# A hybrid decoder layer on one core: expert products in program order, the T5 bias as one row per head, and three more weight chunks requested under the output projection

## The chip, the cores and the metric

The kernel runs on one core of a Trainium2 chip and works in float32 from input to output. The metric is the device time of one execution in microseconds (us): the median of three runs before the change is 1792.37 us (1790.39 to 1792.63). One further execution was recorded by the profiler; it took 1793.54 us, and its recorded span is 1791.8 us. Engines are written as in the profile: PE (TensorE), DVE (VectorE), ACT (ScalarE), POOL (GpSimd), and SP, whose queue issues nearly all loads.

## The reference, cut to what matters

The layer computes 256 tokens plus 16 meta tokens of width 2048:

```python
h = layer_norm(concat([meta, x]))
(mq, mk, mv, mo, mi, mf, aq, ak, av, iq, ik, iw, gm, ga) = split_cols(h @ w_in)
qk = silu(causal_dwconv(concat([mq, mk])))
y_m = mlstm_branch(qk, mv, mo, mi, mf)          # 4 heads
# 8 heads; an indexer keeps 68 keys of 272 for each query
logits = q @ k_sel * scale + rel_bias[t5_bucket(q_pos - sel)]
y_a = softmax(logits) @ v_sel
merged = sigmoid(gm) * (y_m @ w_pm) + sigmoid(ga) * (y_a @ w_pa)
h = layer_norm(ALPHA * h + merged @ w_out)
# 4 groups of 8 experts: one group per token, the two best experts in it
gu = h[tokens of e] @ w_gate_up[e];  y += gate * ((silu(gu[:512]) * gu[512:]) @ w_down[e])
h = layer_norm(ALPHA * h + y);  return h[16:]
```

All 32 experts get their weights read: per expert 8 MB of w_gate_up and 4 MB of w_down.

## The kernel before, in words

**Stages.** In microseconds of the span: the embedding norm and the q/k projections of the mLSTM branch to about 100, the rest of the mLSTM branch to about 180, the indexer and the attention heads to about 400, merge gates and branch projections to about 700, the output projection w_out from 704 to 802, routing to 815, the experts from 815 to 1742, and the last norm to the end.

**Projections.** `fgroup` (L240 ff.) computes 256 columns of a projection. For every 8 rows of 128 it loads 1 MB (`load_w`, L114, on SP, tiles qk_r, mv_r, ...; three tiles in turn), ACT rounds the weights to a high part (L122, qk_00h), DVE takes the rest (L123, qk_00l), and PE multiplies (L261 for high parts, L267 for low). A tile is loaded again when ACT and DVE are done with the load three before it. `bg` is a list of generators: each `step()` moves the first two of them on by one piece, so that small work stands between projections.

**The T5 bias.** `t5_bias` computes for each of 8 heads a row of 400 bias values, in rsb (8 partitions). A DMA on POOL's queue (L310) writes every row 128 times to the DRAM tile rdr. `t5_load` reads it back on SP (L315) with a step of 399 between partitions, so that partition p gets the row shifted by p: the bias matrix Wb, 128 x 272 per head. `attend` adds the mask to Wb on POOL (L565).

**Expert weights.** `specs` lists the transfers of the experts in order: for each pair of experts 16 gate-up chunks of 1 MB, and 8 down chunks of 1 MB of the pair before; `issue(n)` requests the next ones as far as tiles are free or until n are requested. There are 12 free tiles under the output projection (NSLOT), 2 chunks in the tile acc0, and 2 in the tiles of u, which come free when ul is computed. From then on a chunk's tile is given back when its last product is done (`used`). In the output projection, `issue` is called with 4, 6, 8, 8 after the four column blocks; the rest is requested behind it, at `issue(NSLOT + 2)` and `issue(NSLOT + 4)`.

**Experts.** `dispatch(q)` gathers the tokens of four experts by a product with a one-hot matrix (pxe, L1004; 16 row blocks k, each 4 products of 256 columns: two with the high part uh of the tokens, two with the low part ul) and scales them into xe (L1008 on ACT, L1011 on DVE). `up_chunk` has four products of 512 columns per chunk (gu, L1081 and L1083), `down_step` the products py (L1104), and `combine` the products pc (L1212) that add the gated rows to acc. A scheduler orders all instructions of an engine by their priority and readiness; instructions wrapped in `late(...)` keep their place in the program. Before, the expert products aren't wrapped.

The program's own lines of the parts that the change touches:

## Time and profile before

| | value |
|---|---|
| median of three runs | 1792.37 us |
| profiled execution | 1793.54 us |
| its span | 1791.8 us |
| PE busy | 1713.5 us, 96% |
| DVE, ACT, POOL busy | 705.9, 454.1, 115.5 us |
| DMA, mean over the span | 301 GB/s |
| read from HBM | 533.53 MB |

The busy share of PE is a count of recorded matmuls, whose ends are modelled; two matmuls into different column halves of the array overlap in the records. So a busy PE in the experts doesn't by itself say that PE sets the pace there; the DMA share of the same stretch has to be read beside it. The profile's sections give the span in 40 equal slices; the stretches below are finer.

### The profile page before, as it was taken

What the parts mean: (1) busy time and instruction counts of PE and PEld (TensorE: products, weight loads), DVE (VectorE), ACT (ScalarE), POOL (GpSimd) and SP (SyncE); (2) the same over time, 40 slices, a digit from 0 to 9 for tenths busy, and PEclk for the clock granted to TensorE, in tenths of its full rate; (3) what the DMA queues carried; (4) which work ended last, traced back from release to release, by engine and by line L of the source; (5) the groups of instructions that cost most, each with busy time, mean ns of one, the idle gap of its engine ahead of it and who ended that gap; (6) DMA issues with size and microseconds to landing.
All of it is one profiled execution on the core that took longest, in us unless ns stands there. A gap on an engine that the chain in (4) does not pass through costs nothing. (4 is left out here: it accounts for less than half of the span.)

```text
span 1791.8 us, 20692 instructions
## 1 busy us (share of the span) xinstructions
PE 1713.5 (96%) x8478; PEld 1053.3 (59%) x8478; DVE 705.9 (39%) x1180; ACT 454.1 (25%) x687; POOL 115.5 (6%) x139
## 2 busy tenths in 40 slices
PE   8599999999999999999999999999999999999996
PEld 7598899988877877885343443433434434334332
DVE  7356774455456466543123123321222122112215
ACT  5143344444443444334010100100101001001011
POOL 3000200001032022000100000000000000000002
PEclk9799999999998999998999999999999999999998
DMA  7634444447565558648999999999999999999994
GB/s 221 124 124 143 142 154 153 142 149 245 194 196 163 188 189 306 209 168 324 416 393 421 420 419 420 419 419 420 419 419 420 420 419 420 420 420 419 420 411 138
DMA packets 156179, 538.68 MB, mean 301 GB/s; under 512 B 16012, under 2 KB 64356, under 8 KB 107936
## 3 DMA queue, kind: packets, MB, share of 16 engines
q1 hardware_dynamic: 153120, 530.54, 76.8%
q0 software_dynamic: 2896, 6.75, 2.0%
q8 instruction: 68, 1.11, 0.3%
q14 instruction: 31, 0.25, 0.0%
q10 hardware_dynamic: 64, 0.02, 0.0%
HBM read 533.53 MB, written 3.74 MB: 300 GB/s over the span
## 5 line engine op out<-in xcount | busy, mean ns | idle before, releaser
L1081 PE MATMUL gu<-weg,xe 128*64 128x512 f32 x1016 | 465.9, 598 | 0.6 <-DMA weg<-in_w_gate_up_dram 0.6
L1083 PE MATMUL gu<-weg,xe 128*64 128x512 f32 x1016 | 463.6, 598 | 0.0
L1104 PE MATMUL py<-wed,hT 128*64 128x512 f32 x960 | 308.6, 597 | 0.6 <-DMA wed<-in_w_down_dram 0.6
L1081 PEld LDWEIGHTS gu<-weg,xe 128*64 128x64 f32 x1016 | 126.7, 137 | 188.6 <-issue 181.8
L1104 PEld LDWEIGHTS py<-wed,hT 128*64 128x64 f32 x960 | 97.8, 137 | 160.5 <-issue 155.1
L1083 PEld LDWEIGHTS gu<-weg,xe 128*64 128x64 f32 x1016 | 122.3, 136 | 64.9 <-issue 62.7
L1089 ACT ACTIVATE hb<-gu 64x512 f32<-64x512 f32 x32 | 18.9, 592 | 471.4 <-PE gu L1083 471.4
L1090 DVE TENSOR_TENSOR hb<-gu,hb 64x512 f32<-64x512 f32 x32 | 22.0, 689 | 291.1 <-ACT hb L1089 290.5
L1231 DVE SCALAR_TENSOR_TENSOR yl<-py,gsl,yh 128x512 fp32r<-128x512 f32 (+1 forms) x65 | 46.5, 737 | 205.0 <-ACT yh L1230 205.0
L1230 ACT ACTIVATE yh<-py,gsl 128x512 fp32r<-128x512 f32 (+1 forms) x65 | 43.0, 680 | 273.9 <-PE py L1104 201.8
L1218 DVE TENSOR_TENSOR acc<-pc,acc 128x512 f32<-128x512 f32 (+1 forms) x122 | 79.4, 679 | 82.6 <-PE pc L1212 82.5
L1004 PE MATMUL pxe<-oh,uh 128*128 128x256 f32 x256 | 65.5, 333 | 9.0 <-DVE xe L1011 4.8
L1011 DVE TENSOR_SCALAR xe<-pxe,gbp 128x256 f32<-128x256 f32 x64 | 34.8, 544 | 92.4 <-PE pxe L1004 52.1
L1004 PEld LDWEIGHTS pxe<-oh,uh 128*128 128x128 f32 x256 | 40.8, 196 | 47.0 <-DVE xe L1011 15.8
L1204 POOL TENSOR_TENSOR fin<-acc,fin 128x512 f32<-128x512 f32 (+1 forms) x10 | 10.3, 1054 | 896.8 <-DMA wel<-in_w_down_dram 887.2
L1212 PE MATMUL pc<-yh,ohT 128*128 128x512 f32 (+1 forms) x130 | 55.8, 456 | 4.6 <-ACT yh L1230 2.4
L1212 PEld LDWEIGHTS pc<-yh,ohT 128*128 128x128 f32 x130 | 23.1, 191 | 55.5 <-issue 17.8
L1004 PE MATMUL pxe<-oh,ul 128*128 128x256 f32 x256 | 51.6, 284 | 0.0
L1008 ACT ACTIVATE xe<-pxe,gbp 128x256 f32<-128x256 f32 x64 | 36.1, 565 | 59.1 <-PE pxe L1004 58.9
L1212 PE MATMUL pc<-yl,ohT 128*128 128x512 f32 (+1 forms) x130 | 49.1, 405 | 0.8 <-DVE yl L1231 0.7
L1004 PEld LDWEIGHTS pxe<-oh,ul 128*128 128x128 f32 x256 | 40.8, 198 | 0.0
L1212 PEld LDWEIGHTS pc<-yl,ohT 128*128 128x128 f32 x130 | 24.1, 190 | 12.3 <-issue 8.1
(922 smaller groups left out, 3064.3 us busy)
## 6 DMA issues: line engine op xcount, KB each, us to landing
weg<-in_w_gate_up_dram SPq DMA_DIRECT2D x254, 1024.0 KB, 17.7
wed<-in_w_down_dram SPq DMA_DIRECT2D x120, 1024.0 KB, 16.7
gm_r<-in_w_in_dram SPq DMA_DIRECT2D x16, 1024.0 KB, 5.0
ga_r<-in_w_in_dram SPq DMA_DIRECT2D x16, 1024.0 KB, 5.1
wo_r<-in_w_out_dram SPq DMA_DIRECT2D x16, 1024.0 KB, 5.1
qk_r<-in_w_in_dram SPq DMA_DIRECT2D x8, 1024.0 KB, 6.0
mv_r<-in_w_in_dram SPq DMA_DIRECT2D x8, 1024.0 KB, 5.3
aq_r<-in_w_in_dram SPq DMA_DIRECT2D x8, 1024.0 KB, 5.1
```

Of the source, the lines that this page charges most:

```text
L1004: nc.tensor.matmul(pt[:, :4 * C], lhsT=part[:, b, rows_of(k)], rhs=ohf[:, b], start=i == 0 and b == 0, stop=i == 1 and b == 1)
L1008: nc.scalar.activation(xe[:, k], pt[:, :4 * C], AF.Identity, bias=gbp[:, 1, k:k + 1], scale=gbp[:, 0, k:k + 1])
L1011: nc.vector.tensor_scalar(xe[:, k], pt[:, :4 * C], gbp[:, 0, k:k + 1], gbp[:, 1, k:k + 1], op0=ALU.mult, op1=ALU.add)
L1081: nc.tensor.matmul(pg_[other], lhsT=lt, rhs=w[:, kk, 0:512], start=k == 0, stop=k == KD - 1)
L1083: nc.tensor.matmul(pg_[mine], lhsT=lt, rhs=w[:, kk, 512:1024], start=k == 0, stop=k == KD - 1)
L1089: nc.scalar.activation(hb[mine], pg_[other], AF.Silu)
L1090: nc.vector.tensor_tensor(hb[mine], pg_[mine], hb[mine], op=ALU.mult)
L1104: nc.tensor.matmul(py[i * 64:i * 64 + 64], lhsT=hTs[p][:, kk, 64 - i * 64:128 - i * 64], rhs=live["d", 2 * p + i, kk][:, 0, c * 512:c * 51 ...
L1212: nc.tensor.matmul(pc[:, :n], lhsT=ohT[:, b * P:b * P + P], rhs=y[:, :n], start=i == 0, stop=i == 1)
L1218: nc.vector.tensor_tensor(av, pc[:, :n], av, op=ALU.add)
L1230: nc.scalar.activation(yh[:, :n], py[:, :n], AF.Copy, scale=gate)
L1231: nc.vector.scalar_tensor_tensor(yl[:, :n], py[:, :n], gate, yh[:, :n].bitcast(F32), op0=ALU.mult, op1=ALU.subtract)
```

## The change

Five edits:

1. **T5 bias.** rdr holds one row of 400 per head (8 x 400). `t5_load` reads it with a step of one element between partitions, which gives Wb with its partitions in reverse order. A new generator `t5_flip` puts them right: a 128 x 128 matrix with ones on the other diagonal (`anti`), eight float32 products of 128 x 272, and eight copies on ACT back to Wb. It stands in `bg` behind the indexer.
2. **Weights.** A pool `pre` is opened before the output projection. It holds acc0 (chunks 0 and 1 of expert 1) and the tiles yh and yl, which take chunk 7 of expert 0 in four parts of 256 KB. `issue` is called with 4, 8, 10, 10 under the output projection, then NSLOT + 3 and NSLOT + 5.
3. **Dispatch.** Two row blocks share a PSUM bank (`bank`); for the first four experts only two banks are gathered before the first expert product, and one more behind each chunk. The first part of ul is computed on POOL, the others on DVE just before their bank.
4. **Order.** Every product and transpose of the experts is wrapped in `late`. A `combine` comes one step after the gating of its rows (`ready`).
5. **keep_warm** has 11 products instead of 14.

```diff
-    rdr = dram.tile([8, P, 400], F32, name="rdr")
+    rdr = dram.tile([8, 400], F32, name="rdr")
 
...
-        late(nc.gpsimd.dma_start(out=rdr, in_=rsb.unsqueeze(1).to_broadcast([8, P, 400])))
+        late(nc.gpsimd.dma_start(out=rdr, in_=rsb))
 
     def t5_load():
         rv = rdr[:]
         for h in range(0, AH, 2):
             late(nc.sync.dma_start(
                 out=Wb[:, h:h + 2],
-                in_=bass.AP(rv.tensor, rv.offset + h * P * 400 + 127,
-                            [[399, P], [P * 400, 2], [1, L]])))
+                in_=bass.AP(rv.tensor, rv.offset + h * 400, [[1, P], [400, 2], [1, L]])))
+
+    def t5_flip():
+        anti = ap_.tile([P, P], F32, name="anti")
+        nc.gpsimd.memset(anti, 0.0)
+        nc.gpsimd.affine_select(anti, anti, pattern=[[1, P]], compare_op=ALU.not_equal, fill=1.0,
+                                base=1 - P, channel_multiplier=1)
+        yield
+        for h in range(AH):
+            pw = pxt(f"pfl{h}")
+            nc.tensor.matmul(pw[:, :L], lhsT=anti, rhs=Wb[:, h], start=True, stop=True)
+            nc.scalar.copy(Wb[:, h], pw[:, :L])
+            yield
 
 
     qk = mp_.tile([P, 8, L], F32, name="qk")
@@ -605,6 +616,7 @@
             bg.append(g)
 
     bg.append(index_scores())
+    bg.append(t5_flip())
     for j in range(AH // 2):
+            nm = "we" + "_".join(map(str, key))
             if key in extra:
-                w = extra[key]().rearrange("p (a b) -> p a b", a=a)
+                live[key] = extra[key](nm, src)
+                continue
+            home[key] = pool, tag = free.popleft()
+            w = pool.tile([P, a, b], F32, name=nm, tag=tag, bufs=1)
+            nc.sync.dma_start(out=w, in_=src)
+            if key[0] == "g":
+                live[key] = lambda kk, h, w=w: w[:, kk, h * 512:h * 512 + 512]
             else:
-                home[key] = pool, tag = free.popleft()
-                w = pool.tile([P, a, b], F32, name="we" + "_".join(map(str, key)), tag=tag, bufs=1)
-            nc.sync.dma_start(out=w, in_=src)
-            live[key] = w
+                live[key] = w
 
     def used(*key):
     ta_ctx.close()
+    pre = ctx.enter_context(tc.tile_pool(name="pre", bufs=1, side="right"))
+    both = []
+
+    def in_acc(i, nm, src):
+        if not both:
+            both.append(pre.tile([P, 2, 2, 1024], F32, name="acc0", tag="acc"))
+        w = both[0][:, i]
+        nc.sync.dma_start(out=w, in_=src)
+        return lambda kk, h: w[:, kk, h * 512:h * 512 + 512]
+
+    def in_parts(nm, src):
+        ws = [pre.tile([P, 512], F32, name=f"{nm}{i}", tag=("yh", "yl")[i % 2], bufs=2)
+              for i in range(4)]
+        for i, w in enumerate(ws):
+            nc.sync.dma_start(out=w, in_=src[:, i // 2, i % 2 * 512:i % 2 * 512 + 512])
+        return lambda kk, h: ws[2 * kk + h]
+
+    extra.update({("g", 0, 7): in_parts, ("g", 1, 0): lambda *a: in_acc(0, *a),
+                  ("g", 1, 1): lambda *a: in_acc(1, *a)})
     free += [(big, t) for t in YT] + [(mx, t) for t in MT]
     NSLOT = len(free)
-        issue((4, 6, 8, 8)[n])
+        issue((4, 8, 10, 10)[n])
         for b in range(2):
             uv = u[b][:, sl]
             nc.vector.scalar_tensor_tensor(uv, uv, ALPHA, pts[b], op0=ALU.mult, op1=ALU.add)
...
     ul = me.tile([P, 2, D], F32R, name="ul", bufs=1)
-    both = []
-
-    def in_acc(i):
-        if not both:
-            both.append(me.tile([P, 2 * D], F32, name="acc0", tag="acc", bufs=1))
-        return both[0][:, i * D:i * D + D]
-
-    extra.update({("g", 1, NSLOT - 8 + i): lambda i=i: in_acc(i) for i in range(2)})
-    issue(NSLOT + 2)
+    issue(NSLOT + 3)
     free += [(up, t) for t in UT]
 
 
-    keep_warm(14, "warm1")
+    keep_warm(11, "warm1")
     mu1 = cst([P, 2, 2], "mu1")
     rs1 = cst([P, 2], "rs1")
     lg = cst([P, 2, 40], "lg")
...
 
+    def mm(*a, **k):
+        late(nc.tensor.matmul(*a, **k))
+
+    def turned(*a):
+        late(nc.tensor.transpose(*a))
...
         xe = me.tile([P, KD, 4 * C], F32, name=f"xe{q}", tag="xe", bufs=1)
         ohf = oh.rearrange("p b e c -> p b (e c)")
-        for k in range(KD):
-            if q == 0 and k % 4 == 0:
+
+        def bank(kc):
+            if q == 0 and kc % 2 == 0:
                 for b in R2:
-                    sl = slice(k * P, k * P + 512)
-                    nc.vector.tensor_tensor(ul[:, b, sl], u[b][:, sl],
-                                            uh[:, b, sl].bitcast(F32), op=ALU.subtract)
-            pt = pdt(f"pxe{q}_{k}")
-            for i, part in enumerate((uh, ul)):
-                for b in R2:
-                    nc.tensor.matmul(pt[:, :4 * C], lhsT=part[:, b, rows_of(k)],
-                                     rhs=ohf[:, b], start=i == 0 and b == 0,
-                                     stop=i == 1 and b == 1)
-            if k % 2:
-                nc.scalar.activation(xe[:, k], pt[:, :4 * C], AF.Identity,
-                                     bias=gbp[:, 1, k:k + 1], scale=gbp[:, 0, k:k + 1])
-            else:
-                nc.vector.tensor_scalar(xe[:, k], pt[:, :4 * C], gbp[:, 0, k:k + 1],
-                                        gbp[:, 1, k:k + 1], op0=ALU.mult, op1=ALU.add)
-        return xe, ohf
+                    sl = slice(kc * 256, kc * 256 + 512)
+                    if kc == 0:
+                        nc.gpsimd.tensor_tensor(ul[:, b, sl], u[b][:, sl],
+                                                uh[:, b, sl].bitcast(F32), op=ALU.subtract)
+                    else:
+                        late(nc.vector.tensor_tensor(ul[:, b, sl], u[b][:, sl],
+                                                     uh[:, b, sl].bitcast(F32), op=ALU.subtract))
+            pt = pdt(f"pxe{q}_{kc}")
+            for k in (2 * kc, 2 * kc + 1):
+                pv = pt[:, k % 2 * 256:k % 2 * 256 + 256]
+                for i, part in enumerate((uh, ul)):
+                    for b in R2:
+                        mm(pv, lhsT=part[:, b, rows_of(k)], rhs=ohf[:, b],
+                           start=i == 0 and b == 0, stop=i == 1 and b == 1)
+                if k % 2:
+                    nc.scalar.activation(xe[:, k], pv, AF.Identity, bias=gbp[:, 1, k:k + 1],
+                                         scale=gbp[:, 0, k:k + 1])
+                else:
+                    nc.vector.tensor_scalar(xe[:, k], pv, gbp[:, 0, k:k + 1],
+                                            gbp[:, 1, k:k + 1], op0=ALU.mult, op1=ALU.add)
+
+        for kc in range(2 if q == 0 else 8):
+            bank(kc)
+        return xe, ohf, bank
 
     def slots_of(q, ohf):
 
...
 
-    def flush(n=8):
-        for _ in range(min(n, len(pend))):
-            pend.pop(0)()
+    ready = []
+
+    def flush():
+
+        while ready:
+            ready.pop()()
+        if pend:
+            ready.append(pend.pop(0)())
 
     hTs = {}
 
...
-            yh = me.tile([P, 512], F32R, name=f"yh{nn}", tag="yh", bufs=2)
-            yl = me.tile([P, 512], F32R, name=f"yl{nn}", tag="yl", bufs=2)
+            yh = pre.tile([P, 512], F32R, name=f"yh{nn}", tag="yh", bufs=2)
+            yl = pre.tile([P, 512], F32R, name=f"yl{nn}", tag="yl", bufs=2)
             nc.scalar.activation(yh[:, :n], py[:, :n], AF.Copy, scale=gate)
             nc.vector.scalar_tensor_tensor(yl[:, :n], py[:, :n], gate, yh[:, :n].bitcast(F32),
                                            op0=ALU.mult, op1=ALU.subtract)
-            combine(nn, c0, n, yh, yl, cur[0][:, j], p == 0, p == LAST)
+            return lambda: combine(nn, c0, n, yh, yl, cur[0][:, j], p == 0, p == LAST)
         return gated
 
     turn = []
@@ -1244,6 +1291,8 @@
             if kc == 0:
                 pg_ = pgu.tile([P, 512], F32, name=f"gu{e}", tag="gu")
             up_chunk(e, kc, xe, pg_)
+            if p == 0 and n < 6:
+                bank(n + 2)
             while turn:
                 turn.pop()()
             for _ in range(0 if n == 0 else 1 if n < 15 else 2):
             if n == 10 and p % 2:
                 cur = slots_of(p // 2, ohf)
-            if len(pend) > 1 or n < 2:
-                flush(1)
+            flush()
             if n == 7:
                 hb = me.tile([P, 512], F32, name=f"hb{p}", tag="hb", bufs=1)
...
             for i in range(2):
-                nc.tensor.matmul(py[i * 64:i * 64 + 64, :n], lhsT=hTs[LAST][:, kk, 64 - i * 64:128 - i * 64],
+                mm(py[i * 64:i * 64 + 64, :n], lhsT=hTs[LAST][:, kk, 64 - i * 64:128 - i * 64],
                                  rhs=live["l", NE - 2 + i, c0][:, kk], start=kk == 0, stop=kk == 3)
-        gated(c0, n, py)
-    flush()
+        gated(c0, n, py)()
 
     mp_ctx.close()
 
```

Three places in the order of instructions, before and after.

SP's queue under the output projection, before; wo_r are the loads of w_out, weg chunks of w_gate_up, wed of w_down, acc the two chunks in acc0:

```order
L810 DMA weg_6_6649<-in_w_gate_up_dram 128x2048
L114 DMA wo_r_6361<-in_w_out_dram 128x4x512
L114 DMA wo_r_6411<-in_w_out_dram 128x4x512
...
L114 DMA wo_r_6785<-in_w_out_dram 128x4x512
L810 DMA weg_2_6857<-in_w_gate_up_dram 128x2048
L810 DMA weg_0_6853<-in_w_gate_up_dram 128x2048
L810 DMA weg_3_6859<-in_w_gate_up_dram 128x2048
L810 DMA weg_1_6855<-in_w_gate_up_dram 128x2048
L810 DMA weg_7_6651<-in_w_gate_up_dram 128x2048
L810 DMA acc_6861<-in_w_gate_up_dram 128x2048 x2
```

The same place of the changed kernel:

```order
L823 DMA weg_6_6515<-in_w_gate_up_dram 128x2048
L114 DMA wo_r_6393<-in_w_out_dram 128x4x512
L850 DMA weg_70_6517<-in_w_gate_up_dram 128x512
L114 DMA wo_r_6443<-in_w_out_dram 128x4x512
L850 DMA weg_71_6518<-in_w_gate_up_dram 128x512
...
L843 DMA acc_6691<-in_w_gate_up_dram 128x2048
L114 DMA wo_r_6477<-in_w_out_dram 128x4x512
L114 DMA wo_r_6531<-in_w_out_dram 128x4x512
L843 DMA acc_6691<-in_w_gate_up_dram 128x2048
...
L114 DMA wo_r_6826<-in_w_out_dram 128x4x512
L823 DMA weg_5_6900<-in_w_gate_up_dram 128x2048
```

Three chunks (one of them in four parts) have moved from behind the last wo_r load to between the earlier ones; five whole chunks stay behind it.

PE at the first expert products, before; pxe are the gathering products, gu the gate-up products:

```order
L1004 MATMUL pxe0_2_6980<-oh0_6962,ul_6852 128x256 x2
L1081 MATMUL gu0_7077<-weg_0_0_6305,xe0_6965 64x512
L1083 MATMUL gu0_7077<-weg_0_0_6305,xe0_6965 64x512
L1081 MATMUL gu1_7129<-weg_1_0_6853,xe0_6965 64x512
L1083 MATMUL gu1_7129<-weg_1_0_6853,xe0_6965 64x512
L1004 MATMUL pxe0_3_6986<-oh0_6962,uh_6851 128x256 x2
L1004 MATMUL pxe0_3_6986<-oh0_6962,ul_6852 128x256 x2
L1004 MATMUL pxe0_4_6994<-oh0_6962,uh_6851 128x256 x2
L1004 MATMUL pxe0_4_6994<-oh0_6962,ul_6852 128x256 x2
L1004 MATMUL pxe0_5_7000<-oh0_6962,uh_6851 128x256 x2
L1004 MATMUL pxe0_5_7000<-oh0_6962,ul_6852 128x256 x2
L1081 MATMUL gu0_7077<-weg_0_0_6305,xe0_6965 64x512
```

The same place of the changed kernel, where pxe0_1 is the second bank of two row blocks:

```order
L1007 MATMUL pxe0_1_7016<-oh0_6999,uh_6892 128x256 x2
L1007 MATMUL pxe0_1_7016<-oh0_6999,ul_6893 128x256 x2
L1007 MATMUL gu0_7034<-weg_0_0_6337,xe0_7002 64x512 x4
L1007 MATMUL pxe0_2_7041<-oh0_6999,uh_6892 128x256 x2
L1007 MATMUL pxe0_2_7041<-oh0_6999,ul_6893 128x256 x2
L1007 MATMUL pxe0_2_7041<-oh0_6999,uh_6892 128x256 x2
L1007 MATMUL pxe0_2_7041<-oh0_6999,ul_6893 128x256 x2
L1007 MATMUL gu0_7034<-weg_0_1_6339,xe0_7002 64x512 x4
```

The four products of a chunk now stand together, with one bank of eight gathering products between chunks; before, single products of two experts' chunks stood between gathering products.

PE at the end of the experts, before; ph are the transposes of the last pair, pc14 the combination of the pair before, pg broadcast rows, py15 the last pair's down products:

```order
L1083 MATMUL gu31_11137<-weg_31_7_11132,xe7_10725 64x512
L1096 MATMUL ph15_11249<-ident_63,hb15_11134 128x128 x4
...
L1296 MATMUL py15_0_11304<-wel_30_0_11144,hT15_11254 64x512
L1212 MATMUL pc14_15360_11272<-yh14_1536_11268,ohT7_11171 128x512
L1212 MATMUL pc14_15360_11272<-yl14_1536_11269,ohT7_11171 128x512
...
L1296 MATMUL py15_0_11304<-wel_31_0_11146,hT15_11254 64x512
L1296 MATMUL py15_512_11331<-wel_30_512_11148,hT15_11254 64x512
L1212 MATMUL pc15_00_11317<-yh15_0_11313,ohT7_11171 128x512
L1212 MATMUL pc15_01_11324<-yh15_0_11313,ohT7_11171 128x512
L1212 MATMUL pc15_00_11317<-yl15_0_11314,ohT7_11171 128x512
```

The same place of the changed kernel:

```order
L1007 MATMUL gu31_11108<-weg_31_7_11103,xe7_10708 64x512 x4
L1007 MATMUL py14_2_11009<-wed_28_3_11075,hT14_11021 64x512
...
L1007 MATMUL py14_3_11010<-wed_29_3_11077,hT14_11021 64x512
L1007 MATMUL pc14_5120_11210<-yh14_512_11198,ohT7_11142 128x512
...
L1010 MATMUL ph15_11224<-ident_63,hb15_11105 128x128 x4
L1007 MATMUL pc14_10240_11231<-yh14_1024_11218,ohT7_11142 128x512
...
L1007 MATMUL py15_0_11275<-wel_31_0_11117,hT15_11229 64x512
L1007 MATMUL pc15_00_11288<-yh15_0_11284,ohT7_11142 128x512
L1007 MATMUL pc15_00_11288<-yl15_0_11285,ohT7_11142 128x512
```

Four down products and four combination products of the pair before now stand behind the last gate-up chunk, and a block's down products no longer have other work between them.

## Rows read from the trace of the kernel before

**Rows 1.** The page's 40 slices of the span: GB/s

```profile
GB/s 221 124 124 143 142 154 153 142 149 245 194 196 163 188 189 306 209 168 324 416 393 421 420 419 420 419 419 420 419 419 420 420 419 420 420 420 419 420 411 138
```

**Rows 2.** Windows: stretch, its length, busy us (instructions) of PE, PEld, DVE, ACT, POOL, PEclk, DMA share, GB/s

```profile
1100.00:1300.00 200.00, 196.46 (x854) 81.04 (x852) 45.31 (x80) 22.28 (x37) 0.00 (x0) 1.00 1.01 419
```

**Rows 3.** PE in order of time from 1739 us: start, length, what

```profile
1741.71 0.59 PE L1081 MATMUL gu<-weg,xe 128*64 128x512 f32 x1
...
1742.14 0.59 PE L1081 MATMUL gu<-weg,xe 128*64 128x512 f32 x1
```

**Rows 4.** Windows before the experts

```profile
200.00:250.00 50.00, 48.82 (x385) 45.44 (x384) 40.91 (x96) 21.73 (x38) 5.03 (x9) 1.00 0.48 151
250.00:400.00 150.00, 150.00 (x1087) 140.72 (x1086) 73.94 (x146) 67.81 (x136) 9.84 (x15) 1.00 0.49 154
...
700.00:815.00 115.00, 110.96 (x541) 92.90 (x539) 66.79 (x106) 46.96 (x60) 11.59 (x7) 0.97 0.61 214
```

**Rows 5.** PE's waits from 40 to 130 us: total, times, longest

```profile
PE qk_p L261 <- ACT qk_00h L122: 20.3, 1, 20.3
```

**Rows 6.** ACT in order of time, 60 to 84 us: start, length, what [idle before]

```profile
82.05 1.04 ACT L122 CAST qk_00h<-qk_r 128x1024 fp32r<-128x1024 f32 x1 [24.77 <-DMA qk_r<-in_w_in_dram]
```

**Rows 7.** DMA issues from 40 to 60 us: count, KB, median us to landing

```profile
qk_r<-in_w_in_dram SPq DMA_DIRECT2D x3, 1024.0 KB, 32.5
rdr<-rsb POOLq DMA_DIRECT2D x1, 1600.0 KB, 37.6
```

**Rows 8.** DMA from 45 to 79 us: queue, packets, MB, share of 16 engines

```profile
q0 software_dynamic: 439, 1.58, 47.3%
```

**Rows 9.** DMA issues from 36 to 41 us

```profile
qk_r<-in_w_in_dram SPq DMA_DIRECT2D x1, 1024.0 KB, 5.3
mhg<-in_mh_norm_g_dram POOLq DMA_DIRECT2D x1, 512.0 KB, 3.7
```

**Rows 10.** Windows around the wait

```profile
50.60:62.70 12.10, 12.10 (x98) 12.04 (x96) 6.96 (x11) 3.16 (x5) 0.00 (x0) 1.00 0.63 94
62.70:83.15 20.45, 0.16 (x3) 0.00 (x1) 0.02 (x1) 1.10 (x2) 0.00 (x0) 0.57 0.58 109
83.15:98.08 14.93, 14.93 (x97) 14.93 (x97) 9.40 (x13) 5.51 (x7) 0.00 (x0) 0.79 0.57 181
```

**Rows 11.** DMA issues from 148 to 160 us

```profile
Wb<-rdr SPq DMA_DIRECT2D x4, 272.0 KB, 5.8
```

**Rows 12.** PE lines by form, 250 to 400 us: busy us, mean ns | idle

```profile
L567 PE MATMUL pl<-ak,aq 128*128 128x272 f32 x16 | 5.0, 392 | 0.0
```

**Rows 13.** Windows under the output projection and at the start of the experts

```profile
740.00:800.00 60.00, 60.00 (x294) 50.34 (x293) 29.22 (x31) 21.55 (x23) 0.00 (x0) 1.00 0.47 161
...
815.00:840.00 25.00, 24.32 (x120) 12.47 (x122) 9.03 (x23) 9.29 (x18) 0.00 (x0) 0.93 0.70 265
```

**Rows 14.** SP in order of time, 824 to 842 us

```profile
834.20 6.31 SPq L810 DMA_DIRECT2D weg<-in_w_gate_up_dram  x4
```

**Rows 15.** PE in order of time, 812 to 836 us

```profile
817.86 1.12 PE L1081 MATMUL gu<-weg,xe 128*64 128x512 f32 x1
...
820.66 0.51 PE L1004 MATMUL pxe<-oh,uh 128*128 128x256 f32 x2
...
825.44 0.51 PE L1004 MATMUL pxe<-oh,uh 128*128 128x256 f32 x2
...
826.59 0.64 PE L1083 MATMUL gu<-weg,xe 128*64 128x512 f32 x1
```

**Rows 16.** The DMA issued between 838.3 and 838.6 us

```profile
weg<-in_w_gate_up_dram SPq DMA_DIRECT2D x1, 1024.0 KB, 6.6
```

**Rows 17.** PE in order of time in the last block

```profile
1755.63 3.65 PE L1296 MATMUL py<-wel,hT 128*64 128x512 f32 x16
1760.06 0.73 PE L1212 MATMUL pc<-yh,ohT 128*128 128x512 f32 x2 [0.77 <-ACT yh L1230]
```

**Rows 18.** PE's waits from 840 to 1742 us, the longest

```profile
PE ph L1096 <- DVE hb L1090: 9.9, 7, 1.4
```

More of the change, by code (lines that the diff above doesn't have):

```diff
@@ L1021, in slots_of @@
         for j in range(2):
-            nc.tensor.matmul(pr[:, j * S:j * S + S],
+            mm(pr[:, j * S:j * S + S],
                              lhsT=sel[:, 2 * j:2 * j + 2].rearrange("p a b -> p (a b)"), rhs=rkT,
@@ L1030, in slots_of @@
             for b in R2:
-                nc.tensor.matmul(pgt[:, j * 4:j * 4 + 4], lhsT=ohf[:, b, j * P:j * P + P],
+                mm(pgt[:, j * 4:j * 4 + 4], lhsT=ohf[:, b, j * P:j * P + P],
                                  rhs=Gs[:, b, 2 * q + j], start=b == 0, stop=b == 1)
@@ L1080, in up_chunk @@
             lt = xe[:, k, s0:s0 + C]
-            nc.tensor.matmul(pg_[other], lhsT=lt, rhs=w[:, kk, 0:512], start=k == 0,
+            mm(pg_[other], lhsT=lt, rhs=w(kk, 0), start=k == 0,
                              stop=k == KD - 1)
-            nc.tensor.matmul(pg_[mine], lhsT=lt, rhs=w[:, kk, 512:1024], start=k == 0,
+            mm(pg_[mine], lhsT=lt, rhs=w(kk, 1), start=k == 0,
                              stop=k == KD - 1)
@@ L1095, in up_turn @@
         for kk in range(4):
-            nc.tensor.transpose(pt[:, kk * P:kk * P + P], hb[:, kk::4], ident)
+            turned(pt[:, kk * P:kk * P + P], hb[:, kk::4], ident)
         hT = me.tile([P, 4, P], F32, name=f"hT{p}", tag="hT", bufs=1)
@@ L1103, in down_step @@
         for i in range(2):
-            nc.tensor.matmul(py[i * 64:i * 64 + 64], lhsT=hTs[p][:, kk, 64 - i * 64:128 - i * 64],
+            mm(py[i * 64:i * 64 + 64], lhsT=hTs[p][:, kk, 64 - i * 64:128 - i * 64],
                              rhs=live["d", 2 * p + i, kk][:, 0, c * 512:c * 512 + 512],
@@ L1109, in down_step @@
                 used("d", 2 * p + i, kk)
-    xe, ohf = dispatch(0)
-    issue(NSLOT + 4)
+    xe, ohf, bank = dispatch(0)
+    issue(NSLOT + 5)
     acc = rkT = None
@@ L1120, in bcast_rows @@
         r = slice(32 * n, 32 * n + 9)
-        nc.tensor.matmul(pt, lhsT=dg[r], rhs=gr[r], start=True, stop=True)
+        mm(pt, lhsT=dg[r], rhs=gr[r], start=True, stop=True)
         return pt
@@ L1130, in prepare @@
         for b in R2:
-            nc.tensor.transpose(pt[:NE, b * P:b * P + P], rk[:, b], ident)
+            turned(pt[:NE, b * P:b * P + P], rk[:, b], ident)
         nc.vector.tensor_copy(rkT, pt[:NE, :S])
-        acc = me.tile([P, 2, D], F32, name="acc", tag="acc", bufs=1)
+        acc = pre.tile([P, 2, D], F32, name="acc", tag="acc")
     def add_residual(n):
@@ L1140, in add_residual @@
         for b in R2:
-            t = me.tile([P, 512], F32, name=f"rt{n}{b}", tag="yl")
+            t = pre.tile([P, 512], F32, name=f"rt{n}{b}", tag="yl", bufs=2)
             nc.vector.tensor_tensor(t, uh[:, b, sl].bitcast(F32), ul[:, b, sl].bitcast(F32),
@@ L1192, in rows_split @@
         nonlocal gr
-        h = me.tile([P, 512], F32R, name="grh", tag="yh")
+        h = pre.tile([P, 512], F32R, name="grh", tag="yh", bufs=2)
         gr = me.tile([P, 512], F32R, name="gr", bufs=1)
@@ L1211, in combine @@
             for i, y in enumerate((yh, yl)):
-                nc.tensor.matmul(pc[:, :n], lhsT=ohT[:, b * P:b * P + P], rhs=y[:, :n],
+                mm(pc[:, :n], lhsT=ohT[:, b * P:b * P + P], rhs=y[:, :n],
                                  start=i == 0, stop=i == 1)
@@ L1275, in trunk @@
                     turn.pop()()
-                flush()
+                while pend or ready:
+                    flush()
             if q + 1 < NE // 4:
-                xe, ohf = dispatch(q + 1)
+                xe, ohf, _ = dispatch(q + 1)
         if p == 1:
```

1 line of the change is left out of this document (removed).

## The prediction

> **What bounds the kernel now.** I read the GB/s slices first, then windows by stage, then the waits of each stage. The slices show two kernels in one [rows 1]: from about the 21st slice on the memory moves 419 to 421 GB/s without a gap, before that less than half of it mostly. In the experts the DMA share is 1.01 at 419 GB/s [rows 2]; 1 MB takes 1.0486 MB / 419 GB/s = 2.50 us. PE's busy share of 98% there misleads: two gate-up products into different halves start together and the next two 0.43 us later [rows 3], so four experts need 32 chunks x 4 + 16 down chunks x 4 = 192 pairs of products x 0.43 = 82.6 us, and with gathering (64 products, 9.2 us, from 8 in 1.15 us [rows 15]), combining (32 products at about 0.37 us [rows 17]) and some 3 us of small products about 107 us, while their 48 MB take 120 us. The reader is to see that the experts end when the last chunk has come, and that only an earlier start of the stream, or a shorter tail behind it, helps.
>
> Before the experts it is PE. Its windows are full or nearly so [rows 4], so what is cut from PE's path there moves everything behind it forward. The one large hole is early: PE waits once for 20.3 us [rows 5], for a cast on ACT, which itself waited 24.77 us for the load of qk_r [rows 6]. That load and its neighbours took 32.5 us (median of three), beside a write of rdr of 1600 KB that took 37.6 us [rows 7]. The write's queue held 47.3% of the 16 engines from 45 to 79 us while it moved 1.58 MB [rows 8]. A qk_r load just ahead of it landed after 5.3 us [rows 9].
>
> **The T5 edit: the stall.** The write shrinks from 1600 KB to 12.8 KB. The loads then take 5.3 us again [rows 9]: the load that ended at 82.05 was issued by 82.05 - 32.5 = 49.6 and lands by about 55, while PE has work until 62.7 [rows 10]. Gone are the idle 20.45 us, and the lower clock after it: the group that followed took 14.93 us at a granted clock of 0.79 where its like at 1.00 took 12.10 [rows 10], 2.83 us more. Together 23.3 us. What is late next would be ACT, DVE and SP; in the group before, ACT was busy 3.16 and DVE 6.96 of 12.10 us [rows 10], so neither takes the place of the load. If loads come a little late all the same, as much as 4 us of the 23.3 stays; that is the bound I keep for this term, apart from the rivals.
>
> **The T5 edit: the read and the flip.** Wb is read as before with four DMAs of 272 KB, which landed in 5.8 us [rows 11]. They now read all rows from one 12.8 KB block. The nearest row is mhg, 512 KB fetched from a row of 4 KB for each of 128 partitions, in 3.7 us [rows 9], so I take no loss. [...]
>
> The flip adds eight float32 products of 128 x 272 on PE, which stand one by one between projections. The attention's pl products of this shape and type were recorded as 16 records, two each, and 5.0 us of busy time [rows 12], 0.62 us for one. That is eight of them: 5.0 us at most, less what their ends overlap with the next product; I take 4.4. Below, nothing, if they fall into the idle 1.2 us of 200 to 250 and into other waits [rows 4]; above, 6.3, with one wait of 1.3 us for a copy. The eight copies on ACT are hidden: ACT is busy 21.73 of 50 us there. The memset and select on POOL (5.03 of 50 busy) too; if Wb came late, PE would wait at the first flip with all projections queued behind it.
>
> **The weights.** Under the output projection the DMA share is 0.47 over 60 us [rows 13], 32 us free. Three chunks more cost 7.5 us there and cost nothing, unless a wo_r load behind them on SP's queue comes late; one chunk is 2.5 us, and PE shows no idle there to make this a known loss. At the start of the experts the DMA share is 0.70 over 25 us [rows 13]: 7.5 us idle, which is all that can be won. To fill it, tiles must be given back sooner. Before, the third and next tiles were requested from 834.20 on [rows 14], since gathering stood between the products. After: the first gate-up product moves from 817.86 to about 817.3 (three warm-up products and a part of ul less in front), the first chunk is done by 819.0 at full clock or 820.2 at the lower one of this stretch (0.93 [rows 13]; eight products from 817.86 took until 820.66 [rows 15]). Then each chunk costs 4 x 0.43 + 1.15 for a bank, with the clock about 3.0, up to the seventh (838.2), and 1.72 from there on. 17 chunks are requested ahead of any chunk's tile; chunks 7 to 9 give back no tile. So the 25th transfer waits for the eleventh chunk, near 845.5, and lands some 5 us later, 850.5. Before, the 21st was requested at 838.46 and landed 6.6 us later [rows 16], the 25th four times 2.5 later: 855.1. From there the stream is full in both. Difference 4.6; I take 4.4. Bounds: 0 and 7.5.
>
> **Order and tail.** In the experts, waits of PE cost nothing until they use up 120 - 107 = 13 us per four experts. Today's are small (ph 9.9 us in 7 waits over 900 us [rows 18]). The fixed order adds the wait for yh (0.77 [rows 17]) at each of 8 combinations if the step put between doesn't cover it: 6 us, below 13. So nothing, bounds -1 and +8. Behind the last chunk, four down products and four combining products now come before the last pair's blocks: 2 x 0.43 + 4 x 0.37 = 2.3 us, of which 1.4 lies under the wait that stood before ph. Each of five blocks has its products unmixed (3.65 us as in [rows 17]), but then waits for yh and, between the two, for yl: up to 0.4 more each, 2 us; the last combination loses about 1 us of waits. Sum 0.9 + 2 - 1, about +2; I take 1.5, bounds -1 and +5.
>
> **Sum.** 1793.5 - 23.3 + 4.4 - 4.4 + 1.5 = 1771.7 us for an execution like the profiled one. The median lies 1.2 below that execution, so 1770.5; I say 1771.
>
> **Rivals.**
> - *The three chunks fill the whole hole.* If the bank's products run at full clock and SP is never late, the term is 7.5: 1768. For it, the idle 7.5 us; against, the chunks that give back no tile.
> - *A part of the stall stays*, through late loads or a new wait in the mLSTM branch, whose pieces move with it: 5 to 12 us less gain, 1776 to 1783. For it, ACT was idle for 24.77 us too [rows 6] and may have caught up there; against, their shares above.
> - *The block of 12.8 KB is slow to read.* At the pace of the rdr write (1600 KB in 37.6 us) Wb's 1.1 MB takes 26 us, and the next projection's loads wait as qk_r's did, some 20 us: 1791, no change. For it, only that write's pace, which read eight partitions again and again; against, mhg. [...]
> - *The write was not the cause.* Then the loads stay late and 1793.5 + 4.4 - 4.4 + 1.5 = 1795, 1794 against the median. Against it: the loads were slow exactly while queue 0 held half of the engines.
> - *The fixed order makes PE the bound in the experts* (slower). Each of 8 rounds of four experts takes 120 us now. If waits reach 13 us a round they begin to count, and beyond 13 + 21/8 = 15.6 us a round the gain is gone. Twice the wait for yh at each combination, and ph's 1.4 twice, would be 12.3 + 2.8 = 15.1 on its own; with one more per gathering bank (8 x 0.3) it is 17.5, or 8 x 4.5 = 36 us: 1807. Against it: a chunk and a down step stand between gating and combining, over 2 us.
>
> **How the numbers follow.** Forecast within 1766 to 1776: 0.62. Full hole or better: 0.14. A part of the stall stays: 0.13. Slow read 0.04, write not the cause 0.03, PE bound 0.04. The range for 8 in 10 takes the forecast, most of the full hole and most of the remaining stall: 1764 to 1781. A measurement of this kernel tells changes beyond about 0.2% (3.6 us) from none. Faster holds the first three and a little of the slow read: 0.9; within 0.2%, the rest of the slow read and the write that was not the cause: 0.06; slower, the PE bound: 0.04.
>
> **What would show it.** In the profile after: the loads of qk_r near 5.3 us and no wait of PE over 2 us before 100 us with the clock at 1.00; eight products pfl of about 0.5 us each and no wait at them for a DMA; a DMA share above 0.85 in the 25 us behind the first expert product; experts at 419 GB/s as before; and about 13 to 15 us from the last gate-up product to the end of the first of the last pair's blocks. It is wrong if PE waits for qk_r still, if Wb's loads take over 10 us, or if the DMA share in the experts falls below 0.98.

## The result and the profile after

Fifteen runs each: 1780.91 us median (1773.80 to 1787.93) against 1790.48 before (1788.95 to 1793.29); ratio 0.9938, 95% interval 0.9928 to 0.9948. So faster by 9.6 us, clear of noise, but half of the 20 us forecast. The median lies inside the range by luck, 0.1 us below its upper end of 1781; six more runs of the same kernel, below, have 1782.16, outside it. The profiled execution took 1773.80 us with a span of 1772.1, 2.1 us above the 1771.7 summed for it. It is the shortest of the fifteen, though, and the times spread over 14 us where before spread over 4: the profile alone would nearly have confirmed a sum that is wrong in two terms. Three experiments below had one run each of 2151 to 2780 us at a mean granted clock of 0.55 to 0.75, which is left out of their medians and spreads.

The T5 part went as forecast. DMA issues from 30 to 100 us, after:

```profile
mv_r<-in_w_in_dram SPq DMA_DIRECT2D x6, 1024.0 KB, 5.1
qk_r<-in_w_in_dram SPq DMA_DIRECT2D x3, 1024.0 KB, 5.2
rdr<-rsb POOLq DMA_DIRECT2D x1, 12.5 KB, 3.2
```

The loads of qk_r take 5.2 us again, 32.5 before [rows 7]. The block is 12,800 bytes, 12.5 KB as the profile counts. The first product behind the q/k projections (mv_p) starts at 74.7 us, before at 98.1. The windows that answer to [rows 10] have no hole of 20 us and no lower clock; what is idle in the second is one wait of 2.2 us for the gates, which the kernel had before, too:

```profile
50.00:75.00 25.00, 25.00 (x201) 25.00 (x200) 16.62 (x25) 10.71 (x13) 0.00 (x0) 1.00 0.55 174
75.00:100.00 25.00, 22.81 (x183) 22.57 (x182) 15.30 (x26) 13.15 (x22) 0.00 (x0) 1.00 0.29 88
```

The flip, PE lines by form from 150 to 300 us (busy us, mean ns | idle), and the landing of the four Wb loads (min, median, max):

```profile
L327 PE MATMUL pfl<-Wb,anti 128*128 128x272 f32 x16 | 5.7, 438 | 0.0
...
DMA to landing us min/median/max: 5.8/6.1/6.3
```

Eight products with no idle time ahead of them (two records each); Wb's loads took 6.1 us from the 12.5 KB block, 5.8 before [rows 11].

The experts are where it differs. PE's longest waits from 780 to 1720 us, after (total, times, longest):

```profile
PE pxe L1007 <- DVE xe L1050: 42.7, 64, 1.0
PE gu L1007 <- DMA weg<-in_w_gate_up_dram: 30.4, 14, 5.3
PE ph L1010 <- DVE rt L1191: 5.0, 3, 1.9
PE prk L981 <- DVE Ab L977: 2.4, 1, 2.4
```

The first row has 64 waits of 0.67 us; the T5 edit alone, with a bank per row block, has eight waits of this kind there, 4.8 us in all. Where they stand first is in PE's order of time behind the first gate-up product (start, length, what, idle before):

```profile
799.84 0.52 PE L1007 MATMUL pxe<-oh,uh 128*128 128x256 f32 x2
800.19 0.40 PE L1007 MATMUL pxe<-oh,ul 128*128 128x256 f32 x2
801.23 0.51 PE L1007 MATMUL pxe<-oh,uh 128*128 128x256 f32 x2 [0.64 <-DVE xe L1050]
801.58 0.40 PE L1007 MATMUL pxe<-oh,ul 128*128 128x256 f32 x2
801.91 1.94 PE L1007 MATMUL gu<-weg,xe 128*64 128x512 f32 x8
803.77 0.52 PE L1007 MATMUL pxe<-oh,uh 128*128 128x256 f32 x2
```

and in DVE's, where the first half is read:

```profile
800.63 0.54 DVE L1050 TENSOR_SCALAR xe<-pxe,gbp 128x256 f32<-128x256 f32 x1 [4.23 <-PE pxe L1007]
```

Between the two row blocks of one bank PE stands until DVE has read the first half (800.63 + 0.54 = 801.17, and PE goes on at 801.23). A bank and a chunk take 803.77 - 799.84 = 3.93 us. In the windows, the 25 us from the first gate-up product on and the stretch of the experts behind them:

```profile
796.40:821.40 25.00, 21.17 (x96) 9.74 (x96) 7.19 (x19) 5.43 (x12) 0.00 (x0) 0.94 0.71 261
...
836.00:1720.00 884.00, 805.09 (x3679) 312.75 (x3676) 205.96 (x365) 98.43 (x160) 8.31 (x16) 0.98 1.01 419
```

and the 25 us from the first gate-up product on before the change:

```profile
817.86:842.86 25.00, 24.82 (x121) 11.54 (x122) 6.44 (x18) 7.17 (x14) 0.00 (x0) 0.96 0.75 280
```

After the change the DMA share there is 0.71, not above 0.85, and below the 0.75 of before; the window of [rows 13] begins 2.9 us ahead of that product. And in the rest of the experts PE is busy 91% of the time, where before it was 98% [rows 2]: the fixed order puts the two down products of a pair side by side (the 960 records of py are busy 246.4 us, before 308.6), PE gets ahead of the stream and waits for chunks (30.4 us above), and its clock is 0.98 on the mean.

The tail (PE in order of time):

```profile
1736.02 3.65 PE L1007 MATMUL py<-wel,hT 128*64 128x512 f32 x16
1740.46 0.51 PE L1007 MATMUL pc<-yh,ohT 128*128 128x512 f32 x1 [0.79 <-ACT yh L1277]
1741.25 0.51 PE L1007 MATMUL pc<-yl,ohT 128*128 128x512 f32 x1 [0.28 <-DVE yl L1278]
...
1742.15 3.65 PE L1007 MATMUL py<-wel,hT 128*64 128x512 f32 x16
```

A block takes 6.13 us from one py to the next (1736.02 to 1742.15); before, 5.87 (1755.63 [rows 17] to 1761.50). From the last gate-up product to the end of the first block it takes 15.4 us, a little over the 13 to 15 that the prediction named as a sign.

### The profile page after: what moved, and what is told of

Same layout as the page of the kernel before. It is cut to its first block, busy times and chain, and to the rows that moved or that the text cites. A ratio compares the mean times of both kernels' runs of the same rounds, so it can differ in the third digit from the quotient of the medians.

```text
span 1772.1 us, 20945 instructions
## 1 busy us (share of the span) xinstructions
PE 1648.9 (93%) x8488; PEld 1013.8 (57%) x8488; DVE 707.9 (40%) x1178; ACT 457.5 (26%) x695; POOL 118.2 (7%) x143
## 3 DMA queue, kind: packets, MB, share of 16 engines
q1 hardware_dynamic: 153552, 530.54, 77.8%
## 5 line engine op out<-in xcount | busy, mean ns | idle before, releaser
L1007 PE MATMUL gu<-weg,xe 128*64 128x512 f32 x2032 | 495.5, 610 | 30.5 <-DMA weg<-in_w_gate_up_dram 30.4
L1007 PEld LDWEIGHTS gu<-weg,xe 128*64 128x64 f32 x2032 | 140.2, 139 | 312.0 <-issue 246.9
L1007 PE MATMUL py<-wed,hT 128*64 128x512 f32 x960 | 246.4, 597 | 0.0
L1007 PEld LDWEIGHTS py<-wed,hT 128*64 128x64 f32 x960 | 69.6, 139 | 140.1 <-issue 138.7
L1265 DVE TENSOR_TENSOR acc<-pc,acc 128x512 f32<-128x512 f32 (+1 forms) x122 | 78.9, 678 | 88.1 <-PE pc L1007 87.3
L1136 ACT ACTIVATE hb<-gu 64x512 f32<-64x512 f32 x32 | 18.9, 591 | 341.6 <-PE gu L1007 341.6
L1007 PE MATMUL pxe<-oh,uh 128*128 128x256 f32 x256 | 61.1, 321 | 46.1 <-DVE xe L1050 42.7
L1007 PE MATMUL pc<-yh,ohT 128*128 128x512 f32 (+1 forms) x130 | 59.8, 460 | 6.0 <-ACT yh L1277 3.5
L1007 PEld LDWEIGHTS pc<-yh,ohT 128*128 128x128 f32 x130 | 24.7, 190 | 54.9 <-issue 23.8
L1068 DVE TENSOR_SCALAR ohT<-prk,slot 128x512 fp32r<-128x512 f32 x8 | 6.0, 751 | 93.7 <-PE prk L1007 93.7
L760 POOL TENSOR_TENSOR gms<-gms,gas 128x512 f32<-128x512 f32 x8 | 10.9, 1389 | 224.0 <-DVE gas L759 224.0
```

What stands on the lines that cost most here:

```text
L760: nc.gpsimd.tensor_tensor(sg[0][:, b], sg[0][:, b], sg[1][:, b], op=ALU.add)
L1007: late(nc.tensor.matmul(*a, **k))
L1068: nc.vector.tensor_scalar(ohT.rearrange("p a b -> p (a b)"), pr, slot, None, op0=ALU.is_equal)
L1136: nc.scalar.activation(hb[mine], pg_[other], AF.Silu)
L1265: nc.vector.tensor_tensor(av, pc[:, :n], av, op=ALU.add)
```

## The experiments

Stage lengths below are in us of one profiled execution each: prk to gu is from the first prk product (routing) to the first gate-up product, experts from there to the start of the last gate-up product, tail from there to the span's end.

| kernel | median | prk to gu | experts | tail |
|---|---|---|---|---|
| before | 1790.5 to 1791.5 | 4.7 | 924.3 | 49.6 |
| changed (two profiles) | 1780.9, 1782.2 | 7.4, 7.0 | 923.7, 926.2 | 52.0, 52.0 |
| T5 edit alone (two profiles) | 1770.8, 1771.8 | 4.4, 5.4 | 923.2, 924.4 | 49.6, 49.6 |
| all but the T5 edit | 1801.4 | 7.0 | 923.6 | 55.0 |
| changed, experts not in fixed order | 1784.0 | 4.8 | 936.8 | 50.3 |
| changed, a bank per row block | 1775.8 | 6.5 | 920.1 | 56.0 |
| changed, old requests | 1779.4 | 7.0 | 926.2 | 52.0 |
| bank per block, late tiles | 1775.5 | 6.5 | 917.5 | 52.7 |
| and a free tail | 1770.5 | 6.2 | 917.4 | 50.7 |
| and 14 warm-up products | 1768.6 | 6.1 | 917.8 | 50.8 |
| changed, 14 warm-up products | 1782.6 | 7.0 | 928.7 | 53.7 |
| changed, free tail | 1778.2 | 7.4 | 929.2 | 50.0 |

**The changed kernel again.** 

> The changed kernel again, for its spread and a second profile. Its 15 runs lay between 1773.8 and 1787.9 us, where before spread over 4.3 us. Theory A (clock in the experts): the fixed order leaves PE waiting for chunks, the granted clock falls to half for pieces of 3 to 7 us, and a run is long when such a piece falls on the serial work behind the last chunk; expect a median of 1777 to 1784, a spread over 8 us, and in a profile of a longer run the extra time behind the last chunk. Theory B (start of the experts): three fewer warm-up products, the lower clock in the routing stage lasts longer in some runs; expect the same times, with the extra time between 740 and 840 us. Theory C: the T5 edit brings the spread.

1782.16 us (1773.77 to 1786.84), ratio 0.9943 [0.9924, 0.9963]. The second profile, 8.5 us longer, is 6.4 us behind at prk already (4.8 of them by 740 us, in steps), 2.6 more in the experts, and equal in the tail (52.0 both). So the place that theory A names, behind the last chunk, is wrong for this run, and B's place has only a part of it. The two traces show where the 6.4 us come from: PE waits at the same places in both, but behind them the granted clock stays at its lower level longer in the second (of the 1772 windows of 1 us in the first, 1690 have 1.00 and 60 have 0.50). Behind a wait of 2.2 us for the gates its mean is 0.76 from 97 to 104 us (1.00 in the first profile), behind one of 3.1 us for gm_01l it is 0.66 from 546 to 561 us (0.89); the second falls behind by 1.5 and 2.3 us there, by 0.9 in the first 25 us (0.80 against 0.86), and by 1.6 just ahead of prk (0.57 in the last 7.9 us, 1.00 in the first profile). Why one execution has the longer pieces is open.

**The T5 edit alone**, twice.

```diff
-    rdr = dram.tile([8, P, 400], F32, name="rdr")
+    rdr = dram.tile([8, 400], F32, name="rdr")
...
+    bg.append(t5_flip())
```

> Before with the T5 edit alone. Theories A and B: the whole 23.3 us of the stall less the flip come through, 1768 to 1773 us, with a spread of 5 us or less as before, so faster than the complete change. Theory C: a spread over 8 us, 1778 to 1784.

1770.77 us, ratio 0.9885 [0.9868, 0.9902]. 

> Before with the T5 edit alone, again, for its spread on the chip of these runs: 1769 to 1773 us, spread below 5 us. If the stages ahead of the experts vary in it by the 6 us by which they vary between profiles of the changed kernel, the spread is 5 us or more.

 

1771.78 us, ratio 0.9895 [0.9881, 0.9909]; the times spread over 1.6 and 3.3 us. That is -20.2 and -19.7 us, against -23.3 + 4.4 = -18.9 forecast, and theory C falls. The rest of the change gives 10 us of it back.

**All but the T5 edit.**

```diff
-    rdr = dram.tile([8, 400], F32, name="rdr")
+    rdr = dram.tile([8, P, 400], F32, name="rdr")
...
-    bg.append(t5_flip())
```

> The changed kernel with the T5 bias as before (rdr written 128 times, no flip), so the other four edits alone. Theories A and B: slower than before by 5 to 12 us (1796 to 1803), spread over 8 us. Theory C: 1786 to 1791, spread of 5 us or less. My own sum of the prediction without the T5 terms would be -4.4 + 1.5 = 1787.5.

1801.43 us, ratio 1.0065 [1.0052, 1.0077]: the other four edits cost 10.5 us, and the spread is 7.1 us, a little less than A and B expected. -19.7 + 10.5 = -9.2, the whole result (-9.6): the parts add up.

**Expert products not in program order.**

```diff
     def mm(*a, **k):
-        late(nc.tensor.matmul(*a, **k))
+        nc.tensor.matmul(*a, **k)
```

> The changed kernel with the expert products not held in program order; all else as changed. Theory A: PE waits less for chunks, the clock stays up in the experts, 1768 to 1774 us, spread 5 us or less. Theory B: like the changed kernel, 1777 to 1784 with a spread over 8 us.

1783.95 us, ratio 0.9966 [0.9953, 0.9979]. Neither: the spread shrinks to 5 us and prk to gu falls to 4.8, since the scheduler fills the waits in one bank with the other (PE's waits for DVE's xe are 7.1 us in all, 42.7 in the changed kernel), but the experts take 936.8. With the old order and the shared banks PE holds up the stream: the 25th request on SP comes 37.0 us behind the first gate-up product (34.1 in the changed kernel), and the memory's rate falls to 326, 368 and 356 GB/s in three windows of 22 us from 906, 1038 and 1148 us, with PE busy 21.75 us or more of each. The T5 edit alone has one such window (364 GB/s), the changed kernel none. So the fixed order by itself isn't what costs time in the middle; with shared banks it saves 10 us or more there.

**A bank per row block.**

```diff
-            pt = pdt(f"pxe{q}_{kc}")
             for k in (2 * kc, 2 * kc + 1):
-                pv = pt[:, k % 2 * 256:k % 2 * 256 + 256]
+                pv = pdt(f"pxe{q}_{k}")[:, :256]
```

> The changed kernel, but each row block k of the gathering gets a PSUM bank of its own again (as before); order, loads and the rest as changed. Theory D (shared bank): in a shared bank PE waits 0.64 to 0.7 us for DVE to read the first half before it may write the second, 64 times and 42.7 us in all; eight of these stand in a row with the first chunks, where a chunk and bank take 3.94 us instead of about 3.0, so tiles come back late. Then the waits of pxe for xe fall below 10 us, the 21st request comes 4 to 5 us sooner after the first gate-up product, and the median is 1774 to 1778. Theory E (loads): the start is late because three early chunks lie in tiles that are not given back, so the bank changes little: 1779 to 1783.

1775.82 us, ratio 0.9912 [0.9898, 0.9927], as D has it, and PE's waits for xe fall to 4.8 us. The 21st request comes 2.3 us sooner (15.7 us behind the first gate-up product instead of 17.9), not 4 to 5; the 25th comes 5.0 sooner. PE in order of time, its second and third bank behind the first gate-up product:

```profile
803.41 0.52 PE L1007 MATMUL pxe<-oh,uh 128*128 128x256 f32 x2
803.76 0.40 PE L1007 MATMUL pxe<-oh,ul 128*128 128x256 f32 x2
804.00 0.40 PE L1007 MATMUL pxe<-oh,uh 128*128 128x256 f32 x2
804.24 0.40 PE L1007 MATMUL pxe<-oh,ul 128*128 128x256 f32 x2
804.57 1.94 PE L1007 MATMUL gu<-weg,xe 128*64 128x512 f32 x8
806.44 0.52 PE L1007 MATMUL pxe<-oh,uh 128*128 128x256 f32 x2
```

806.44 - 803.41 = 3.03 us per bank and chunk, the 3.0 that the prediction used. The 25th request on SP stands 29.0 us behind the first gate-up product (825.53 - 796.49), before 26.6 (844.48 - 817.86), and in the changed kernel, whose row is this, 34.1 (830.47 - 796.40):

```profile
830.47 0.33 SPq L823 DMA_DIRECT2D weg<-in_w_gate_up_dram  x1
```

Its tail is longer (56.0) by a piece of lower clock:

```profile
1716.50:1756.00 39.50, 33.11 (x132) 13.00 (x128) 20.45 (x43) 7.80 (x13) 9.38 (x9) 0.91 0.42 149
```

The changed kernel has 1.00 in the same place (1720 to 1758 us), and PE is busy there for 29.92 us instead of 33.11: 3 us of 4 are that.

**Old requests.**

```diff
-        issue((4, 8, 10, 10)[n])
+        issue((4, 6, 7, 7)[n])
```

> The changed kernel with 4, 6, 7, 7 chunks requested under the output projection instead of 4, 8, 10, 10: the three chunks in the pool pre are requested only behind it. Theory D: the request of the three chunks early is worth little, since tiles that come back limit the stream: within 2 us of the changed kernel (1779 to 1784). A rival: the early chunks are worth up to three times 2.5 us, so this is 1785 to 1789.

1779.43 us, ratio 0.9931 [0.9918, 0.9945]. The 25th request is 34.0 us behind the first gate-up product, as in the changed kernel. Asking for three chunks under the output projection is worth nothing here: tiles that come back set the pace of the stream, not what was loaded ahead.

**Late tiles.** The tiles that are not given back take chunks 13 to 15 of the first pair, on top of the bank per block.

```diff
-    extra.update({("g", 0, 7): in_parts, ("g", 1, 0): lambda *a: in_acc(0, *a),
-                  ("g", 1, 1): lambda *a: in_acc(1, *a)})
+    extra.update({("g", 1, 5): lambda *a: in_acc(0, *a), ("g", 1, 6): lambda *a: in_acc(1, *a),
+                  ("g", 1, 7): in_parts})
...
```

These three chunks are also put into the eighth to tenth place of the requests.

> As the one with a bank for each row block, and the tiles that are not given back (acc0, yh and yl) take chunks 5, 6 and 7 of expert 1 (13 to 15 of the first pair) instead of chunks 7 to 9; these are requested under the output projection in the same places. Theory E: chunks 7 to 9 now give back their tiles at once, the 25th transfer is requested three chunks of 1.72 us sooner, and the median is 3 to 5 us below that of the one before. Theory D alone: no more than 1 us. With both, 1770 to 1775.

1775.53 us, ratio 0.9910 [0.9897, 0.9923]. The medians can't tell it from the one before, so the 3 to 5 us of theory E didn't come. The stage has a part of them: experts 917.5 after 920.1, and the 25th request 23.8 us behind the first gate-up product (820.03 - 796.24) instead of 29.0, what three chunks are worth. Of these 5.2 us the stream keeps half: the 40th transfer lands 72.0 us behind the first gate-up product instead of 74.2, and the two kernels below with the same tiles have 71.6 and 71.9, and experts of 917.4 and 917.8. There is one profile without late tiles to set against these three.

**A free tail**, on both, and alone.

```diff
...
             if p == LAST:
+                strict.append(lambda i: i)
```

> As the one before, with the products behind the last gate-up chunk not held in program order. The stretch from the landing of the last gate-up chunk to the end of the span is 52.2 us in the kernel before with the T5 edit, 54.9 in the changed one; expect 52 to 53 and a median 2 to 3 us below the one before, 1768 to 1773. If the tail's length comes from a lower clock instead of the order, no change.

1770.54 us, ratio 0.9882 [0.9868, 0.9896].

> The changed kernel with the products behind the last gate-up chunk not held in program order, nothing else. The stretch from the last gate-up product to the end of the span is 49.6 us in both kernels with the old order and 52.0 in the changed one; expect 49.6 to 51 and a median of 1778 to 1779. If no change: 1780 to 1783.

1778.20 us, ratio 0.9936 [0.9922, 0.9951]. The tail falls by 2.0 us in both profiles (52.7 to 50.7, 52.0 to 50.0): the order costs 2 us there. From the landing of the last gate-up chunk, as the first expectation counts, it is 2.0 in the first (55.6 to 53.6, so not 52 to 53) and 0.3 in the second (54.9 to 54.6), where PE uses up the last chunks 1.7 us later; its mean granted clock is 0.79 from 1712 to 1720 us there. The first median fell by 5.0 us, more than the tail; the rest of that isn't explained. The second kernel keeps a spread of 7 us.

**Warm-up.**

```diff
-    keep_warm(11, "warm1")
+    keep_warm(14, "warm1")
```

> The one with a bank per block, late tiles and a free tail, with 14 warm-up products instead of 11. Theory F (warm-up): with 11, PE stands idle 2.4 us ahead of prk and the first gathering runs at the lower clock (from prk to the first gate-up product 6.2 to 7.4 us, before 4.7); with 14 the idle time goes below 1.5 us, that stretch falls to about 5 us, and the median by 1 to 2 us, to 1768 to 1770. If the lower clock there doesn't come from the idle time: no change, 1770 to 1772.

1768.56 us, ratio 0.9872 [0.9858, 0.9886].

> The changed kernel with 14 warm-up products again, nothing else. Theory F: 1 to 2 us below the changed kernel's 1781, 1778 to 1780. Otherwise within its interval, 1779 to 1783.

1782.55 us, ratio 0.9943 [0.9930, 0.9957]. Theory F falls: PE no longer waits ahead of prk, but prk to gu stays at 6.1 and 7.0, and neither time moves beyond its interval. That stretch is long because the fixed order puts two whole banks, four row blocks, ahead of the first gate-up product, where three stood before: with these four in banks of their own it still takes 6.1 to 6.5 us, and with the scheduler's order, which again puts three ahead, 4.8. Taking the shared banks away saves 0.9 us of it (7.4 to 6.5). This last profile, 1785.1 us of span, shows what a long run is made of. Windows in its experts:

```profile
1600.00:1640.00 40.00, 34.05 (x139) 19.39 (x136) 11.72 (x19) 8.44 (x14) 0.00 (x0) 0.74 0.96 398
```

and the memory's rate in the 40 slices of 1600 to 1680 us (2 us each):

```profile
GB/s 414 434 414 418 426 406 426 414 426 414 422 422 414 434 414 418 373 229 344 291 319 270 238 389 426 414 430 410 434 414 442 410 430 410 426 426 385 438 410 426
```

PE was at the lower clock for 20 us of the first 40; the stream fell below 345 GB/s for 12 us, as chunks were used up slowly and their tiles came back late (SP waited up to 13.6 us for a product gu from 1560 to 1680 us, in the changed kernel up to 6.6), and the landings are 3 us later from there on. The profile of the changed kernel with a free tail has a second such piece, 20.5 us from 1489 us on at a granted clock of 0.50, and landings 2 us later. The profile of before has only one piece of 4 us in the experts (0.50 from 1448 to 1451 us).

The kernel with a bank per block, late tiles, free tail and 14 warm-up products is the fastest of all: 1768.56 us, below before by 1.3% and, comparing ratios, at the edge of the T5 edit alone (0.9872 against 0.9885 and 0.9895; the intervals overlap).

## Why the prediction was right and where it was wrong

**The stall (-23.3) and the flip (+4.4): right.** Both together measured -20.2 and -19.7 against -18.9. In the traces the stall is 23.4 us at the first mv_p product (98.1 to 74.7), 22.9 with the T5 edit alone, and the stretch with the flip, from the first aq_p to the first av0p product, grows by 3.7 us (44.3 to 48.0). The write of rdr was the cause, and nothing else took the place of the late loads. The slow-read rival falls with 6.1 us for Wb's loads: 1.1 MB came from 12.5 KB within about 8 us, where that rival, at the pace of the rdr write, had 26. (The four loads were issued from 130.3 to 132.0 us and took up to 6.3 us each to land.)

**The weights (-4.4): the step that failed.** The prediction walked the tiles that come back with "4 x 0.43 + 1.15 for a bank, with the clock about 3.0". It took the gathering's products as unbroken, as they stood before, where each row block had a bank. The diff puts two into one, and PE then waits 0.64 us in each for DVE to read the first half. At 3.93 instead of 3.0, six chunks with a bank make 5.6 us, and the first chunk took 3.4 instead of 2.9; the 25th request came 34.1 us behind the first gate-up product, where the walk had 845.5 - 817.3 = 28.2, so 5.9 late. (Four chunks of 1.72 behind 838.2 would be 845.1, a slip of 0.4.) With the wait taken away it is 29.0. Ahead of the first gate-up product the change puts four row blocks where three stood, in two shared banks: the prediction moved that product 0.5 us earlier, and it came 2.5 us later after prk. So instead of -4.4 the term is about +2.5 ahead of the first gate-up product, 0 for the early requests, and a late start of the stream that the experts win back only in part: the 40th transfer lands 77.8 and 78.9 us behind the first gate-up product in the two profiles of the changed kernel, 74.6 and 75.8 with the T5 edit alone.

**Order and tail (+1.5): mis-sized.** The tail is 2.4 us longer, and 2.0 come back when it is freed. In the middle the order costs nothing by waits: PE keeps ahead of the stream, though the rival's 13 us a round were eaten into (64 shared-bank waits are 5.3 us a round). What was not foreseen stands beside that slack: in the kernels whose PE waits for chunks the granted clock is at the lower level in six to nine pieces of the experts, mostly of 3 to 8 us, twice of 20.

**The sum.** The four edits beside T5 were put at -2.9 and measured +10.5 without T5, about +10 with it. Four profiles (the changed kernel twice, old requests, 14 warm-up products) against the two of the T5 edit alone split this, as means: 2.2 us ahead of prk, 2.2 from prk to gu, 2.4 in the experts, 2.8 in the tail, together 9.6. In single profiles of the changed kernel and its nearest kin the experts take 923.7 to 929.2. The 2.2 ahead of prk aren't shown to be the change's: profiles of one program differ by 6 us there (789.0 and 795.4 us), by pieces of lower clock, and the T5 edit alone has profiles 3.5 us apart. The single edits agree: the bank is worth 5 us, the tail's order 2, early requests and warm-up products nothing that can be told. Of the rivals, the full hole, the slow read and another cause of the stall are refuted by the T5 edit alone and by the 25th request. PE as the bound in the experts is refuted for the fixed order, and without it found only at the start and in three short windows (936.8 us). The time fell where a part of the stall was to stay (1776 to 1783), but not by that: the stall is gone, and the time is lost mostly from routing on. So the range held the result for a reason that it wasn't drawn for.

## What to carry to other kernels

Two results in one PSUM bank made the second's products wait until the first was read, in a fixed order of products (64 waits of 0.67 us); count that wait wherever the bank stands in a row with what frees the next load. Whether the chip needs it, or only the program's own order of accesses to a tile, was not tried. Chunks loaded ahead were worth nothing here (the 25th request 34.1 us behind the first gate-up product with three more of them, 34.0 without) while tiles that come back set the pace; tiles that aren't given back are best filled with the chunks that are needed last, which was worth 2 to 3 us in the experts and didn't show in the median. And when one edit carries nearly all of a gain, time it alone before judging the rest: here it was worth twice the whole.

## What the runs showed of the hardware

- One write of 1600 KB from eight partitions on POOL's queue held 47.3% of the 16 DMA engines over 34 us [rows 8], and 1 MB loads on SP's queue took 32.5 us beside it, 5.2 without it; as 12.5 KB it takes 3.2 us.
- Four reads of 272 KB each, into 128 partitions, took hardly longer out of 12.5 KB than out of 1600 KB: 6.1 against 5.8 us from issue to landing (medians).
- The granted clock fell in the experts in six to nine pieces in each profile of the changed kernel and of those with its order (eight in the first of the changed kernel, to 0.50 from 1.00, with PE 91% busy there); before and with the T5 edit alone, PE 98% busy, there was at most one, and with the experts not in fixed order, 97%, there were three. A piece of 20 us cost the DMA stream 2 to 3 us, in two profiles. That such pieces make the spread isn't shown: the two fastest kernels have eight and nine of them, and their four runs each spread by 2.7 and 3.0 us.
